# A hybrid decoder trunk on one NeuronCore: where on the queue the stored attention outputs come back, and which engine makes one sum

## The chip, the cores and the metric

One Trainium2 chip (trn2), one of its cores. The metric is the device time of one execution in microseconds (us), the median of several runs. The engines of the core are named as the profile names them: PE is TensorE (PEld its weight loads), DVE is VectorE, ACT is ScalarE, POOL is GpSimd, SP is SyncE, whose sequencer issues nearly all DMAs (SPq).

## The reference

Two layers on a sequence of 1024 tokens with 1024 features: a recurrent layer (RG-LRU) and a stick-breaking attention layer with 16 heads of 64, each followed by a dense feed-forward block. The change lies in attention:

```python
def stick_breaking_attention(x, w_qkv, w_o):
    qkv = jnp.einsum("bsd,de->bse", x, w_qkv).reshape(bsz, seq, 3, N_HEADS, HEAD_DIM)
    ...
    for blk in range(seq // Q_BLOCK):
        ...
        z = jnp.einsum("bhqd,bhkd->bhqk", qb, kb).astype(jnp.float32) * scale
        ...
        log_fail = jnp.where(strict, jax.nn.log_sigmoid(-z), 0.0)
        suffix = lax.cumsum(log_fail, axis=3, reverse=True) - log_fail
        weights = jnp.where(strict, jnp.exp(jax.nn.log_sigmoid(z) + suffix), 0.0)
        outs.append(jnp.einsum("bhqk,bhkd->bhqd", weights.astype(vb.dtype), vb))
    ...
    return jnp.einsum("bse,ed->bsd", o, w_o)
```

## The kernel before

**Tiles.** The activations lie transposed: 8 row blocks of 128 features (index k or d) by two column blocks of 512 tokens (index n). Each float32 matrix product is made of three matmuls of a high and a low part (mm3, lines 142 to 145). The input of attention lies in the tiles xh[k][n] and xl[k][n], 256 KB each. In the profile and in the listings below, these tiles carry the names of the buffers that they lie over: vh, vl or xg with numbers. xh[0][0] is vh0_3_2532 and xl[0][0] is vl0_3_2533; xh[1][0] and xl[1][0] are xg0_6477 and xg1_6478; xh[4][0] and xl[4][0] are vh2_3_2536 and vl2_3_2537.

**Attention.** The 16 heads go in 8 pairs (q from 0 to 7, NP = 8), each with its two heads hx. For each pair a projection makes q, k and v (which = 0, 1, 2) from all eight row blocks of xh and xl, for n = 0 and then n = 1 (qkv_steps; its matmuls write qk_ps). Each head has its score matmuls (z_ps, lines 1680 and 1681, in two PSUM buffers), a sigmoid on ScalarE (L1693), a running product on VectorE (scan, L1700 and L1703), and a transpose of the weights: partly by PE (wt_ps, L1725), with a cast th by ScalarE and a remainder tl by VectorE (L1734, L1735), partly by DMA (wt<-wx, L1714, whose operand wx ScalarE and VectorE write in L1710 and L1711). The matmuls av_ps (L1748) apply them. After each group a copy and an addition collect the two heads (oo, L1759 and L1760), add_v adds the values (oo<-oo,vt, L1764), and the result is split again into a high and a low part (L1771, L1772).

**Stored outputs.** The output of pair q belongs in row block q of the input of the next product, w_o. But xh and xl hold the input of attention until the last projection, that of v of pair 7. So the outputs of the first pairs are stored to DRAM (od[q, n]: odh and odl) and brought back into xh[q][n] and xl[q][n]. bring_back appends their two loads to a list, back.

**Order.** All five engines' orders are written out here. The loop over u runs through 192 units of work, 12 for each head, one step each: it carries out tasks whose time has come (due; stage(task, n) puts a task n steps ahead), issues one load from back (two in some of the last steps, L1870), makes scores and scans, then av_ps and transposes, then two steps of the running projection, and, from a few steps before pair 7's own heads, pieces of the product with w_o (out_fill, written as ob in the profile, then ob_ps). ob uses row blocks 0 to 6 of n = 0 in turn. SP's queue keeps the order in which the DMAs were written, and an instruction that waits holds up those behind it. Weight loads for what follows attention (raw<-in_attn_w_o, L116, 512 KB) are partly placed among them by the scheduler of the part behind.

The loads of pairs 0 to 5 are put on the list in the second half of evacuate, once the last projection of a column block n is complete (lines 1610 to 1612).

Of the kernel before, what the change touches and what calls it, by code (L numbers as in the profile page):

```python
# [34 lines left out]
def trunk(  # L35
# [21 lines left out]
    nc = tc.nc  # L57
# [84 lines left out]
    def mm3(ps, wh, wl, mh, ml, first, last, **kw):  # L142
        nc.tensor.matmul(ps, lhsT=wh, rhs=mh, start=first, stop=False, **kw)  # L143
        nc.tensor.matmul(ps, lhsT=wh, rhs=ml, start=False, stop=False, **kw)  # L144
        nc.tensor.matmul(ps, lhsT=wl, rhs=mh, start=False, stop=last, **kw)  # L145
# [1326 lines left out]
    NP = HEADS // 2  # L1472
# [15 lines left out]
    with ExitStack() as st:  # L1488
# [25 lines left out]
        def bring_back(*which):  # L1514
            for q, n in which:
                for x, dst in enumerate((xh, xl)):
                    back.append((f32(dst[q][n]), od[q, n][x]))


        def stage(task, steps=1):  # L1520
            soon.append([steps, task])

        def load_link(i):
            q, which = divmod(i, 3)
            if q < NP:
                raws[i] = load_raw(cols(w_qkv, which * D + q * P), (ND,))
            else:
                mix[0].load(which)
# [42 lines left out]
        def qkv_steps(q):  # L1571
            for which in range(3):
                w, at = wq.pop((q, which)), 3 * q + which + 1
                if at < 3 * NP:
                    raw = raws.pop(at)
                    wq[divmod(at, 3)] = next_weights(raw)
                    if which == 1:
                        later.extend(column_norms(raw, q))
                else:
                    mix[0].w[mix[0].order[0]] = next_weights(mix[0].raw.pop(0))  # L1580
                for i in (at + 1,) if at < 3 * NP else (at + 1, at + 2):
                    load_link(i)

                ks = (1, 5, 2, 6, 3, 7, 0, 4) if (q, which) == (0, 0) else range(ND)
                for n in range(NH):
                    pool, tag = (psZ, "z") if (q, which) == (0, 0) else (psQ, "qk")
                    ps = pool.tile([P, NB], F32, tag=tag, name="qk_ps")
                    for i, k in enumerate(ks):
                        mm3(ps, w[0][:, k], w[1][:, k], xh[k][n], xl[k][n], i == 0, i == ND - 1)
                        if i < ND - 1:  # L1590
                            yield
                    ev = evacuate(q, which, n, ps)
                    next(ev)
                    yield
                    next(ev, None)


        def evacuate(q, which, n, ps):
            full = lambda tag, m: [ap.tile([P, m, S], F32R, tag=tag, name=tag, bufs=4 if m == 1 else 3) for _ in range(2)]
            cs = slice(n * NB, (n + 1) * NB)  # L1600
            if which == 2:
                if n == 0:
                    VT[q] = ap.tile([P, S + 1], F32, tag="vt", name="vt", bufs=2)
                    nc.gpsimd.memset(VT[q][:, 0:1], 0.0)
                    VV[q] = ap.tile([P, 2, NT, 2, HD], F16, tag="v", name="v", bufs=2)
                t = ap.tile([P, NB], F32, tag="t", name="t", bufs=1)
                after = VT[q][:, n * NB + 1 : (n + 1) * NB + 1]
                nc.vector.scalar_tensor_tensor(after, ps, f32(sv[q]), rbc[n], op0=ALU.mult, op1=ALU.mult)
                yield
                if q == NP - 1:  # L1610
                    some = [(p, n) for p in range(NP - 2)]
                    bring_back(*some[:3], *([(NP - 2, 0)] * n), *some[3:])
                nc.vector.tensor_sub(t, VT[q][:, cs], after)
                vx = ap.tile([P, 4, 2, P], F16, tag="vx", name="vx", bufs=2)
                t3 = t.rearrange("p (b c) -> p b c", b=4)

                def low():
                    nc.vector.scalar_tensor_tensor(
                        vx[:, :, 1], t3, 1 / UP, vx[:, :, 0], op0=ALU.mult, op1=ALU.subtract
                    )  # L1620
                    for hx, a in enumerate((top, bot)):
                        nc.sync.dma_start(
                            VV[q][:, hx, 4 * n : 4 * n + 4].rearrange("p b h c -> p (b h) c"),
                            vx[a].rearrange("p b h c -> p (b h c)"),
                            transpose=True,
                        )
                def high():
                    nc.scalar.activation(vx[:, :, 0], t3, AF.Copy, scale=1 / UP)
                    stage(low)

                stage(high, 2)
                return
            two = ap.tile([P, 2, NB], F32R, tag="two", name="two", bufs=2)

            def spread():
                for hx, (a, b) in enumerate(((top, bot), (bot, top))):
                    if which == 0:
                        nc.sync.dma_start(f32(Q[q][hx])[a, cs], f32(two)[a, 0])
                        nc.sync.dma_start(f32(Q[q][hx])[b, cs], f32(two)[a, 1])
                    else:  # L1640
                        for half_ in (top, bot):
                            nc.sync.dma_start(f32(KK[q][hx])[half_, :, cs], f32(two)[a])

            def low():
                nc.vector.tensor_sub(two[:, 1], t, f32(two)[:, 0])
                stage(spread)

            if which == 0:
                t = ps
                if n == 0:  # L1650
                    Q[q] = [x[:, 0] for x in full("q", 1)]
                nc.scalar.copy(two[:, 0], t)
                yield
                low()
            else:
                t = f32(two)[:, 1]
                nc.vector.tensor_mul(t, ps, rbc[n])
                if n == 0:
                    KK[q] = full("kk", 2)
                yield  # L1660

                def high():
                    nc.scalar.copy(two[:, 0], t)
                    stage(low)

                stage(high)
# [73 lines left out]
        def av_part(tht, q, hx, G, kb, first, last):  # L1740
            q0 = (max(kb, 4 * G) - 4 * G) * P
            if first:
                av[0] = psO.tile([P, NB], F32, tag="o", name="av_ps")
            ps = av[0]
            if tht is None:
                tht = [T[q, hx][:, 2 * kb + x].rearrange("p j c -> p (j c)") for x in range(2)]
            for x, t in enumerate(tht):
                nc.tensor.matmul(  # L1748
                    ps[:, q0:], lhsT=VV[q][:, hx, kb], rhs=t[:, q0:], start=first and x == 0, stop=last and x == 1
                )  # L1750
            if not last:
                return
            a, b = (top, bot)[:: 1 if hx == 0 else -1]

            def gather():
                if hx == 0:
                    oo[q, G] = ap.tile([P, NB], F32, tag="oo", name="oo", bufs=2)
                o = oo[q, G]
                nc.scalar.copy(o[a], ps[b])  # L1759
                nc.vector.tensor_add(o[a], ps[a], o[a])  # L1760

            def add_v():
                eng = nc.vector if q >= NP - 2 else nc.gpsimd
                eng.tensor_add(oo[q, G], oo[q, G], VT[q][:, G * NB + 1 : (G + 1) * NB + 1])  # L1764

            def parts():
                o = oo[q, G]
                down = f32(av_[q])

                def both(hi, lo):  # L1770
                    nc.scalar.activation(hi, o, AF.Copy, scale=down)  # L1771
                    nc.vector.scalar_tensor_tensor(lo, o, down, f32(hi), op0=ALU.mult, op1=ALU.subtract)  # L1772

                if not kept(q, G):
                    both(xh[q][G], xl[q][G])
                else:
                    oh = ap.tile([P, NB], F32R, tag="oh", name="oh", bufs=1)
                    both(oh, o.bitcast(F32R))

                    def store():  # L1780
                        nc.sync.dma_start(od[q, G][0], f32(oh))
                        nc.sync.dma_start(od[q, G][1], o)

                    stage(store)

            later.insert(0, gather)
            if hx == 1:
                later.extend((add_v, lambda: None, parts))
# [32 lines left out]
        with tc.manual_schedule(engines={E.PE, E.Activation, E.DVE, E.Pool, E.SP}):  # L1821
# [39 lines left out]
            for u in range(-LEAD, len(units)):  # L1861
                some = chunks[c : c + 1]
# [92 lines left out]
```

## Time and profile before

| | us |
|---|---|
| median of 3 runs | 2152.64 |
| lowest and highest run | 2151.5, 2154.63 |
| the profiled execution | 2151.32 |
| its span, first to last instruction | 2149.3 |
| TensorE busy | 2127.2 (99% of the span) |
| VectorE busy | 1778.7 (83%) |
| ScalarE busy | 1136.3 (53%) |
| GpSimd busy | 129.0 (6%) |

Rows of the profile read: start in us from the span's start, duration in us, engine, line, operation, out<-in with the shape, how many were merged, and in brackets the idle time of the engine just before and what ended it. Rows of the waits read: who waited for whom, us in total, how often, the longest. In the rows of the stages, the pairs are busy time and count of PE, PEld, DVE, ACT and POOL, then the clock that TensorE was granted (1.00 is full), the mean busy share of the 16 DMA engines, and GB/s. A row of SPq is the issue of a DMA, not its transfer. GpSimd's additions of attention (L1764) are 12 in number with a mean of 1610 ns; the four that VectorE makes take 667 to 694 ns.

### The profile page before, as it was taken

What the parts mean: (1) busy time and instruction counts of PE and PEld (TensorE: products, weight loads), DVE (VectorE), ACT (ScalarE), POOL (GpSimd) and SP (SyncE); (2) the same over time, 40 slices, a digit from 0 to 9 for tenths busy, and PEclk for the clock granted to TensorE, in tenths of its full rate; (3) what the DMA queues carried; (4) which work ended last, traced back from release to release, by engine and by line L of the source; (5) the groups of instructions that cost most, each with busy time, mean ns of one, the idle gap of its engine ahead of it and who ended that gap; (6) DMA issues with size and microseconds to landing.
All of it is one profiled execution on the core that took longest, in us unless ns stands there. A gap on an engine that the chain in (4) does not pass through costs nothing. (4 is left out here: it accounts for less than half of the span.)

```text
span 2149.3 us, 28075 instructions
## 1 busy us (share of the span) xinstructions
PE 2127.2 (99%) x10158; PEld 1742.8 (81%) x10158; DVE 1778.7 (83%) x2609; ACT 1136.3 (53%) x1838; POOL 129.0 (6%) x100
## 2 busy tenths in 40 slices
PE   8999999999999999999999999899999999999998
PEld 7888888888888888888777777668888888888887
DVE  7887768888888888896899899877888888888886
ACT  6567435444444545564666666544544444454556
POOL 1222020000000000000000000002000000000002
PEclk9999999999999999999999999999999999999999
DMA  7111422334445774536667677972234444586442
GB/s 236 49 50 39 155 96 64 116 111 155 138 154 169 275 231 136 161 119 145 140 149 151 153 156 157 216 235 96 70 109 127 153 133 156 187 276 227 134 155 90
DMA packets 390314, 315.45 MB, mean 147 GB/s; under 512 B 101272, under 2 KB 296992, under 8 KB 390176
## 3 DMA queue, kind: packets, MB, share of 16 engines
q1 hardware_dynamic: 390016, 313.40, 49.9%
q8 instruction: 79, 1.29, 0.2%
q14 instruction: 59, 0.48, 0.1%
q10 hardware_dynamic: 160, 0.27, 0.0%
HBM read 184.09 MB, written 83.36 MB: 124 GB/s over the span
## 5 line engine op out<-in xcount | busy, mean ns | idle before, releaser
L143 PE MATMUL p_ps<-vh,wbh 128*128 128x512 f32 x524 | 204.9, 391 | 0.0
L144 PE MATMUL p_ps<-vl,wbh 128*128 128x512 f32 x524 | 204.5, 390 | 0.0
L143 PE MATMUL p_ps<-vh,wch 128*128 128x512 f32 x524 | 204.2, 390 | 0.0
L145 PE MATMUL p_ps<-vh,wcl 128*128 128x512 f32 x524 | 204.1, 389 | 0.0
L145 PE MATMUL p_ps<-vh,wbl 128*128 128x512 f32 x524 | 203.9, 389 | 0.0
L144 PE MATMUL p_ps<-vl,wch 128*128 128x512 f32 x524 | 203.9, 389 | 0.0
L722 ACT CAST wbh<-sb 128x1024 fp32r<-128x1024 f32 (+2 forms) x69 | 69.6, 1009 | 191.6 <-DVE sb L702 191.6
L1693 ACT ACTIVATE w<-z_ps,rs 128x128 f32<-128x128 f32 (+1 forms) x192 | 110.9, 580 | 100.1 <-PE z_ps L1681 99.8
L145 PE MATMUL p_ps<-vh,wal 128*128 128x512 f32 x396 | 154.0, 389 | 0.0
L143 PE MATMUL p_ps<-vh,wah 128*128 128x512 f32 x396 | 154.0, 389 | 0.0
L144 PE MATMUL p_ps<-vl,wah 128*128 128x512 f32 x396 | 154.0, 389 | 0.0
L1700 DVE TENSOR_TENSOR_SCAN w<-w,unit 128x128 f32<-128x128 f32 (+3 forms) x128 | 104.9, 830 | 17.4 <-ACT w L1693 17.1
L145 PEld LDWEIGHTS p_ps<-vh,wbl 128*128 128x128 f32 x524 | 98.4, 188 | 21.1
L145 PEld LDWEIGHTS p_ps<-vh,wcl 128*128 128x128 f32 x524 | 98.4, 188 | 21.0 <-DVE wcl L736 0.6
L144 PEld LDWEIGHTS p_ps<-vl,wch 128*128 128x128 f32 x524 | 98.4, 188 | 20.5
L143 PEld LDWEIGHTS p_ps<-vh,wch 128*128 128x128 f32 x524 | 98.3, 188 | 20.5 <-ACT tb L1181 0.2
L143 PEld LDWEIGHTS p_ps<-vh,wbh 128*128 128x128 f32 x524 | 98.6, 188 | 19.7 <-ACT U L1181 0.4
L144 PEld LDWEIGHTS p_ps<-vl,wbh 128*128 128x128 f32 x524 | 98.6, 188 | 18.5
L143 PE MATMUL qk_ps<-vh,whi 128*128 128x512 f32 x264 | 111.9, 424 | 0.0
L145 PE MATMUL qk_ps<-vh,wlo 128*128 128x512 f32 x264 | 103.6, 392 | 0.0
L144 PE MATMUL qk_ps<-vl,whi 128*128 128x512 f32 x264 | 103.3, 391 | 0.0
L143 PE MATMUL p_ps<-vh,wd 128*128 128x512 f32 x254 | 99.4, 391 | 0.1
(402 smaller groups left out, 5796.3 us busy)
## 6 DMA issues: line engine op xcount, KB each, us to landing
raw<-in_ffn_w_in SPq DMA_DIRECT2D x88, 512.0 KB, 4.1
vl<-pd SPq DMA_DIRECT2D x128, 256.0 KB, 3.5
pd<-U SPq DMA_DIRECT2D x90, 256.0 KB, 2.3
kk<-two SPq DMA_DIRECT2D x64, 256.0 KB, 4.5
raw<-in_ffn_w_out SPq DMA_DIRECT2D x56, 256.0 KB, 3.6
raw<-in_attn_w_qkv SPq DMA_DIRECT2D x24, 512.0 KB, 5.4
h<-hd SPq DMA_DIRECT2D x32, 256.0 KB, 5.4
hd<-h SPq DMA_DIRECT2D x32, 256.0 KB, 2.0
```

The lines of the kernel that those rows point to most:

```text
L143: nc.tensor.matmul(ps, lhsT=wh, rhs=mh, start=first, stop=False, **kw)
L144: nc.tensor.matmul(ps, lhsT=wh, rhs=ml, start=False, stop=False, **kw)
L145: nc.tensor.matmul(ps, lhsT=wl, rhs=mh, start=False, stop=last, **kw)
L722: nc.scalar.copy(self.full(self.wb), self.full(self.sb))
L1693: nc.scalar.activation(F, ps[:, 0:n], AF.Sigmoid, scale=rs[:, j : j + 1])
L1700: nc.vector.tensor_tensor_scan(rev, rev, unit[:, NB - n :][:, ::-1], 0.0, op0=ALU.mult, op1=ALU.add)
```

## The change

A stored row block k of column block n is now put on the list two steps after the last projection's matmuls for k and n were written, not for all k together when the projection of n is complete. Row block 6 of n = 0, which is stored late, follows block 3 of n = 1. And the addition of the values for pair 6 goes to GpSimd, like those of pairs 0 to 5; only pair 7's stays on VectorE.

```diff
@@ qkv_steps
                     for i, k in enumerate(ks):
                         mm3(ps, w[0][:, k], w[1][:, k], xh[k][n], xl[k][n], i == 0, i == ND - 1)
+                        if (q, which) == (NP - 1, 2):
+                            if k < NP - 2:
+                                stage(lambda k=k, n=n: bring_back((k, n)), 2)
+                            if (n, k) == (1, 3):
+                                stage(lambda: bring_back((NP - 2, 0)), 2)
                         if i < ND - 1:
                             yield
@@ evacuate
                 yield
-                if q == NP - 1:
-                    some = [(p, n) for p in range(NP - 2)]
-                    bring_back(*some[:3], *([(NP - 2, 0)] * n), *some[3:])
                 nc.vector.tensor_sub(t, VT[q][:, cs], after)
@@ add_v
-                eng = nc.vector if q >= NP - 2 else nc.gpsimd
+                eng = nc.vector if q == NP - 1 else nc.gpsimd
```

The order of PE's and ScalarE's instructions is the same in both kernels. SP's queue before, from the transpose for which SP waits at 1365.63 us to the load of the second row block (kk is the keys of pair 7; v the transposes of its values):

```order
L1714 DMA_TRANSPOSE wt_12375<-wx_12372 128x8x128
L1642 DMA kk_12224<-two_12294 64x2x512 x2
L1642 DMA kk_12225<-two_12294 64x2x512 x2
L1714 DMA_TRANSPOSE wt_12375<-wx_12413 128x8x128
L1714 DMA_TRANSPOSE wt_12375<-wx_12438 128x8x128
L1870 DMA vh0_3_2532<-odh0_0_7885 128x512
L1714 DMA_TRANSPOSE wt_12375<-wx_12480 128x8x128
L1870 DMA vl0_3_2533<-odl0_0_7886 128x512
L1622 DMA_TRANSPOSE v_12429<-vx_12445 128x8x64 x2
L1870 DMA xg0_6477<-odh1_0_7887 128x512
L1870 DMA xg1_6478<-odl1_0_7888 128x512
```

The same place of the changed kernel:

```order
L1872 DMA vh0_3_2532<-odh0_0_7885 128x512
L1716 DMA_TRANSPOSE wt_12376<-wx_12373 128x8x128
L1644 DMA kk_12224<-two_12294 64x2x512 x2
L1644 DMA kk_12225<-two_12294 64x2x512 x2
L1872 DMA vl0_3_2533<-odl0_0_7886 128x512
L1716 DMA_TRANSPOSE wt_12376<-wx_12415 128x8x128
L1872 DMA xg0_6477<-odh1_0_7887 128x512
L1716 DMA_TRANSPOSE wt_12376<-wx_12441 128x8x128
L1872 DMA xg1_6478<-odl1_0_7888 128x512
L1716 DMA_TRANSPOSE wt_12376<-wx_12483 128x8x128
L1872 DMA vh4_3_2540<-odh2_0_7889 128x512
L1624 DMA_TRANSPOSE v_12431<-vx_12448 128x8x64 x2
```

The first load moved ahead of all four transposes, its partner ahead of three, and the loads of the second row block stand among them.

SP's queue before, around the loads of the fifth row block (vh2 and vl2; odh6 and odl6 are stores of pair 6):

```order
L1870 DMA xg9_7656<-odl3_0_7892 128x512
L116 DMA raw_13150<-in_attn_w_o 128x8x128
L1622 DMA_TRANSPOSE v_12429<-vx_12554 128x8x64 x2
L1781 DMA odh6_0_7897<-oh_12581 128x512
L1782 DMA odl6_0_7898<-oo_12213 128x512
L1870 DMA vh2_3_2536<-odh4_0_7893 128x512
L1870 DMA vl2_3_2537<-odl4_0_7894 128x512
L1870 DMA xg4_6481<-odh5_0_7895 128x512
```

And in the changed kernel:

```order
L1872 DMA xg9_7656<-odl3_0_7892 128x512
L1872 DMA vh2_3_2536<-odh4_0_7893 128x512
L1872 DMA vl2_3_2537<-odl4_0_7894 128x512
L1872 DMA xg4_6481<-odh5_0_7895 128x512
L1624 DMA_TRANSPOSE v_12431<-vx_12557 128x8x64 x2
L1783 DMA odh6_0_7897<-oh_12584 128x512
L1784 DMA odl6_0_7898<-oo_12213 128x512
L1872 DMA xg5_6482<-odl5_0_7896 128x512
```

The three loads moved ahead of the transposes and stores, and the weight load raw_13150 is gone from here; it now stands behind the last of the loads that come back, between the transposes of the last head.

GpSimd's queue at the end of attention, as the difference of the two (vt are the values, wlo a part of a weight):

```order
 L1548 TENSOR_SCALAR sv<-nh 128x1
 L1549 TENSOR_SCALAR av<-nh 128x1
-L1604 MEMSET vt 128x1
+L1609 MEMSET vt 128x1
+L1766 TENSOR_TENSOR oo<-oo,vt 128x512 x2
 L1559 TENSOR_TENSOR wlo<-raw,whi 128x512 x2
```

Two additions are new there. On VectorE the two rows oo<-oo,vt of pair 6 are gone, and nothing else of its order is different.

## The prediction

> **What bounds the kernel now.** First the page's list of engines, then the waits of TensorE between 1370 and 1425 us, the stretch in which attention ends and the stored outputs come back.
>
> ```profile
> PE 2127.2 (99%) x10158; PEld 1742.8 (81%) x10158; DVE 1778.7 (83%) x2609; ACT 1136.3 (53%) x1838; POOL 129.0 (6%) x100
> ...
> PE ob L144 <- DMA vl<-odl: 2.7, 2, 2.4
> PE ob L143 <- DMA vh<-odh: 2.7, 2, 2.4
> PE av_ps L1748 <- DVE tl L1735: 2.2, 4, 0.8
> PE av_ps L1748 <- ACT th L1734: 2.2, 2, 1.7
> ```
>
> TensorE (PE) is busy 99% of the span, so the change can win only where PE stands or runs slowly. Here it stands 5.4 us for loads of the stored outputs (columns of the waits: us in total, times, longest). Next the busy time by stage; behind the engines stand the granted clock, the share of the DMA engines and GB/s.
>
> ```profile
> 1363.40:1366.90 3.50, 3.50 (x19) 2.42 (x18) 3.28 (x6) 2.99 (x7) 1.62 (x3) 1.00 0.02 5
> 1366.90:1381.00 14.10, 11.47 (x64) 8.61 (x62) 14.04 (x23) 7.82 (x17) 0.00 (x0) 1.00 1.04 202
> 1381.30:1384.70 3.40, 3.40 (x11) 1.87 (x10) 3.15 (x6) 2.97 (x5) 0.00 (x0) 0.50 0.88 235
> ...
> 1391.10:1394.90 3.80, 1.09 (x4) 0.49 (x4) 3.39 (x7) 1.70 (x4) 0.00 (x0) 1.00 0.99 282
> 1394.90:1398.30 3.40, 3.40 (x12) 2.37 (x12) 0.78 (x2) 1.04 (x4) 0.00 (x0) 0.50 1.14 258
> 1398.30:1410.00 11.70, 10.35 (x59) 6.81 (x58) 11.39 (x18) 7.87 (x16) 0.00 (x0) 1.00 1.02 333
> 1421.00:1440.00 19.00, 19.00 (x93) 14.40 (x92) 11.36 (x17) 8.81 (x14) 0.00 (x0) 1.00 0.84 266
> ```
>
> Three things stand in it. Two stretches of 3.4 us have half the clock, each just behind a wait for a load. VectorE (DVE, third pair) is full almost everywhere: 14.04 of 14.10, 11.39 of 11.70. It has real holes only where PE stood for the second load. And the DMA engines are free from 1363.4 to 1366.9 and then full until 1410. After 1421 PE never stops (19.00 of 19.00), so whatever is won by then stays won.
>
> So the question is which engine ends the waits at each place. PE's rows:
>
> ```profile
> 1380.92 0.51 PE L144 MATMUL ob<-vl,whi 128*128 128x512 f32 x1 [2.43 <-DMA vl<-odl]
> ...
> 1382.71 0.80 PE L1680 MATMUL z_ps<-kk,q 128*128 128x512 f32 x1
> ...
> 1393.52 0.49 PE L143 MATMUL ob<-vh,whi 128*128 128x512 f32 x1 [2.40 <-DMA vh<-odh]
> ...
> 1397.04 0.85 PE L1725 MATMUL wt_ps<-ident,w 128*128 128x128 f32 x3
> ...
> 1381.56 0.63 ACT L1628 ACTIVATE vx<-t 128x512 f16<-128x512 f32 x1 [3.38 <-DVE t L1613]
> 1382.10 0.56 ACT L1693 ACTIVATE w<-z_ps,rs 128x384 f32<-128x384 f32 x1
> ...
> 1401.87 0.73 ACT L1771 ACTIVATE vh<-oo,av 128x512 fp32r<-128x512 f32 x1
> ```
>
> The score matmul z_ps at 1382.71 needs one of two PSUM buffers, which the sigmoid at 1382.10 empties (it ends at 1382.66). That sigmoid is queued behind vx, which waits for DVE's t. **So the first wait hides a second one**: with its load early, PE would run on for about 1.8 us and stand at the score matmul until 1382.5. The second wait has no such thing behind it. VectorE's rows:
>
> ```profile
> 1379.13 1.22 DVE L1700 TENSOR_TENSOR_SCAN w<-w,unit 128x512 f32<-128x512 f32 x1
> 1380.26 0.67 DVE L1764 TENSOR_TENSOR oo<-oo,vt 128x512 f32<-128x512 f32 x1
> 1380.84 0.69 DVE L1613 TENSOR_TENSOR t<-vt 128x512 f32<-128x512 f32 x1
> ...
> 1390.52 1.16 DVE L1735 TENSOR_TENSOR tl<-wt_ps,th 128x512 f16<-128x512 f32 x2 [0.36 <-ACT th L1734]
> ...
> 1398.12 0.62 DVE L1735 TENSOR_TENSOR tl<-wt_ps,th 128x256 f16<-128x256 f32 x2 [2.62 <-ACT th L1734]
> ...
> 1399.37 0.69 DVE L1760 TENSOR_TENSOR oo<-av_ps,oo 64x512 f32<-64x512 f32 x1
> ...
> 1400.97 0.67 DVE L1764 TENSOR_TENSOR oo<-oo,vt 128x512 f32<-128x512 f32 x1
> 1401.67 1.16 DVE L1735 TENSOR_TENSOR tl<-wt_ps,th 128x512 f16<-128x512 f32 x2
> ...
> 1404.19 0.73 DVE L1772 SCALAR_TENSOR_TENSOR vl<-oo,av,vh 128x512 fp32r<-128x512 f32 x1
> ```
>
> VectorE is idle 0.36 and 2.62 us for th, ScalarE's cast of PE's transposed weights, which PE made late because it stood for loads. Those holes, not PE's 5.4 us, are what earlier loads can win.
>
> **The change part by part. The loads.** Their number and size stay; they move on SP's one queue.
>
> ```profile
> 1356.85 2.42 SPq L116 DMA_DIRECT2D raw<-in_attn_w_o  x2
> 1365.63 1.26 SPq L1714 DMA_TRANSPOSE wt<-wx  x1
> ...
> 1375.46 1.26 SPq L1714 DMA_TRANSPOSE wt<-wx  x1
> 1376.77 0.57 SPq L1870 DMA_DIRECT2D vl<-odl  x1
> ...
> 1383.45 0.42 SPq L116 DMA_DIRECT2D raw<-in_attn_w_o  x1
> ...
> 1389.79 0.39 SPq L1870 DMA_DIRECT2D vh<-odh  x1
> ```
>
> SP stands from 1359.3 (1356.85 + 2.42) to 1365.63 for that transpose's operand. The first load now stands ahead of it, so it goes out at about 1359.3 and falls into the free 3.5 us. Its partner passes two transposes. That ends the 2.43 us wait, but by the rows above PE then stops at 1382.5 instead of 1382.7: nearly nothing. The fifth pair, issued at 1389.79, passes the 512 KB weight load of 1383.45, two transposes and two stores; it takes the weight load's place behind the fourth pair, so it is issued at about 1383.5, 6 us earlier. Needed at 1391.1 (1393.52 - 2.40), or some 2 us before that in a schedule that runs ahead, it has 5 to 7 us to land; vl at 1376.77 took 4.1 (to 1380.92). So the 2.40 us wait ends. The weight load goes to the back, where nothing of PE's needs it before 1421.
>
> *(a) holes.* 0.36 at 1390.52 (bounds 0 and 0.36). Of the 2.62 at 1398.12 I take 2.55, as the casts still follow a wait of ScalarE for the scan ahead (bounds 0, should the pair land late, and 2.62). Cover: PE's transposes of 1397.04 come 2.4 us earlier without the wait, and 1.0 or more without the half clock around them: at 1393.6 or before. VectorE, working without holes, gets to tl only at about 1395. So a load may be 1.4 us late there at no cost, and beyond that costs what it is late.
>
> **The sum on GpSimd.** Two additions of 0.67 us leave VectorE; the same additions of earlier heads show what they do there.
>
> ```profile
> 1323.43 0.75 DVE L1608 SCALAR_TENSOR_TENSOR vt<-qk_ps,sv,rbc 128x512 f32<-128x512 f32 x1
> 1323.48 1.10 POOL L1764 TENSOR_TENSOR oo<-oo,vt 128x512 f32<-128x512 f32 x1 [13.36 <-DVE oo L1760]
> ...
> 1324.09 1.56 DVE L1700 TENSOR_TENSOR_SCAN w<-w,unit 128x512 f32<-128x512 f32 x1
> 1325.58 0.66 DVE L1613 TENSOR_TENSOR t<-vt 128x512 f32<-128x512 f32 x1
> ...
> 1341.48 2.12 POOL L1764 TENSOR_TENSOR oo<-oo,vt 128x512 f32<-128x512 f32 x1 [16.90 <-DVE oo L1760]
> ...
> 1342.63 1.52 DVE L1711 TENSOR_TENSOR wx<-w,wx 128x512 f16<-128x512 f32 x1
> ```
>
> *(b) first addition.* Beside it the scan took 1.56 instead of 1.22. From scan to t it was 1325.58 - 1324.09 = 1.49 with the sum on GpSimd; now it is 1380.84 - 1379.13 = 1.71. Won: 0.22 (bounds 0 and 0.58, the slot of the addition). The instructions of VectorE around it are the same ones, so 0.22 it is.
>
> *(c) second addition.* Its slot is 1401.67 - 1400.97 = 0.70. GpSimd took 2.12 in the like place, and a two-input operation beside it 1.52 where it takes about 0.68: up to 0.84 given back. VectorE's next instruction here reads PSUM, like vt at 1323.43, which was not stretched. So less is given back than that: won 0.45 (bounds -0.14 and 0.70). The sum is also ready later: GpSimd ends 2.12 after oo is ready, against 1401.64 - 1400.06 = 1.6 now, so ScalarE's vh (1401.87) and the casts queued behind it slip by 0.5. VectorE reads vh only at 1404.19, 1.6 after it is written, which hides that; without this cover it costs 0.5.
>
> A rule of the Trainium skill speaks against this edit: its page "SBUF — State Buffer", section "SBUF: two separate sides", says that VectorE with two SBUF inputs and GpSimd exclude one another for a whole instruction. By it both additions cost VectorE about what they free, and the sum below would lose 0.6; the stretched scan agrees in kind, at 0.34 of it.
>
> *(d) half clock.* The two half-clock stretches are charged to the holes only as far as they fell on them in this execution. Where they lie relative to the waits can differ from run to run; half of 3.4 us is 1.7 us for one that is all in the way, and I add a quarter of it, 0.4 (bounds 0 and 1.7).
>
> "TensorE: Matmul & The Clock Gate" in the Trainium skill, section "Part 1: The HAM clock gate", has the clock halved after an idle window of about 3.4 us. The rows show it behind waits of 2.4 us, so the measurement decides; by the page's number term (d) would be 0.
>
> **Sum:** 0.36 + 2.55 + 0.22 + 0.45 + 0.4 = 3.98, about 4.0 us. The profiled execution took 2151.3 us (its span is 2149.3), so 2147.3 for it. It lies 1.3 us under the median of the runs, 2152.64, from which the forecast is **2148.6 us**.
>
> **The rivals.** *All of PE's loss comes back.* 5.4 us of waits and two half-clock stretches (3.4 us lost) are 8.8 us: 2143.8. For it: PE is 99% busy. Against: VectorE's 14.04 of 14.10 and the score matmul behind the first wait. It holds if VectorE catches up faster than its rows say.
>
> *The loads land no earlier.* From 1366.9 on the DMA engines are full, and a new order moves no more bytes. Then one load in the free stretch, (b) and (c) are left: about 1.0 us, 2151.6. Against: what the fifth pair passes is 512 KB and four other transfers, which nobody awaits.
>
> *Slower: transposes pushed back.* Transposes two to four of the head in work there now stand behind one, two and three loads. If each holds the full queue for half of vl's 4.1 us (an estimate), three take 6.2, and the fourth transpose goes out at 1375.46 + 6.2 = 1381.7 and lands 4.1 later, at 1385.8. PE takes it just behind the score matmul of 1382.5, at about 1383. It decides from there: PE would stand 2.8 us and lose 1.7 more at half clock, the holes of (a) would stay, and the end would be 2157.1. Against: the load itself costs SP only 0.57, and with that alone the transpose lands at 1381.3, 1.7 us in time.
>
> **How the numbers follow.** Forecast 0.59, full recovery 0.15, no earlier 0.18, transposes 0.08. The forecast's own range is 2147.0 to 2150.2. The range 2145.0 to 2153.0 takes in the no-earlier case and some of the full recovery; it leaves out the transposes and the rest. A measurement of this kernel can tell about 0.2%, 4.3 us, from no change; that line is at 2148.3, just beside the forecast. Faster: 0.15 and about half of 0.59, 0.43. Slower: most of the last case, 0.07. Within: 0.50.
>
> **What would show it.** Right: no TensorE wait of ob for a load over 0.5 us at the first pair, and in its place a wait of z_ps of some 2.5 to 3 us that ends at about 1382.5; no hole over 0.3 us of VectorE ahead of tl between 1385 and 1400; the tl of 1398.12 at about 1395; GpSimd additions of about 1.1 and 2.1 us, the scan beside the first at about 1.55; attention's last matmuls some 4 us earlier. The forecast is wrong if PE's av_ps waits for a transpose, if the fifth pair is still awaited for over 1.5 us, or if a new wait of VectorE for ScalarE stands around 1398, behind the second sum.

## The result and the profile after

| | before | after |
|---|---|---|
| median, us | 2152.44 (22 runs) | 2148.89 (22 runs) |
| lowest and highest run | 2149.77, 2155.22 | 2146.85, 2151.5 |
| the profiled execution, and its span | 2151.32, 2149.3 | 2150.7, 2148.9 |

The ratio is 0.9983, with a 95% interval of 0.9977 to 0.9990: 3.55 us, 0.17%, won. That is clear of no change, and just under the 0.2% (2148.3 us) that the prediction set as its line. The forecast was 2148.6 us, its own range 2147.0 to 2150.2, and the time lies in it. The wide range, 2145.0 to 2153.0, is little of a test, since it takes in the time of the kernel before.

The two profiled executions are only 0.6 us apart, since they are not typical ones: the one of before lies 1.1 us under its median, the one of after 1.8 us above. The one of after was already 1.15 us late at the last projection, long before the change has any effect (the matmul at 1344.26 starts at 1345.41), and lost another 0.6 us behind attention, at about 2112 us. All times of after around 1370 to 1420 are therefore to be read minus 1.15.

First, the engines and the waits of TensorE between 1370 and 1425 us in the profile after (who waited for whom: us in total, times, the longest).

```profile
PE 2126.3 (99%) x10158; PEld 1741.3 (81%) x10158; DVE 1778.8 (83%) x2607; ACT 1135.9 (53%) x1838; POOL 125.6 (6%) x102
...
PE z_ps L1682 <- ACT w L1695: 3.6, 3, 2.9
PE ob L143 <- DMA vh<-odh: 2.4, 1, 2.4
PE av_ps L1750 <- DVE tl L1737: 1.9, 3, 0.9
PE ob L144 <- DMA xg<-odl: 1.0, 1, 1.0
```

The loads are awaited for 3.4 us instead of 5.4, and at other places; the wait of z_ps for ScalarE's sigmoid was 0.2 us before and is 3.6 now. The stages, cut as before (busy time and count of PE, PEld, DVE, ACT and POOL, clock, DMA share, GB/s):

```profile
1363.40:1366.90 3.50, 3.50 (x19) 2.37 (x18) 3.31 (x6) 2.87 (x6) 1.71 (x3) 1.00 0.64 201
1366.90:1381.00 14.10, 13.60 (x74) 10.31 (x72) 13.97 (x23) 8.94 (x19) 1.09 (x1) 1.00 1.03 214
1381.30:1384.70 3.40, 1.09 (x5) 0.68 (x6) 3.15 (x6) 2.25 (x5) 0.00 (x0) 1.00 0.68 154
...
1394.90:1398.30 3.40, 2.94 (x20) 1.95 (x19) 2.92 (x7) 3.35 (x8) 0.21 (x1) 1.00 1.34 276
1398.30:1410.00 11.70, 7.46 (x32) 3.76 (x32) 10.98 (x16) 6.84 (x15) 1.59 (x1) 0.96 0.98 282
```

The free 3.5 us of the DMA engines are now used (0.64 instead of 0.02). Both half-clock stretches are gone from their places. VectorE works in 1394.9 to 1398.3, where it had done 0.78. But PE has lost ground in 1398.3 to 1410 (7.46 instead of 10.35), and its clock is 0.96 there: a new half-clock stretch begins at 1409.13. PE's and ScalarE's rows show why:

```profile
1379.24 0.40 PE L143 MATMUL ob<-vh,whi 128*128 128x512 f32 x1
...
1383.61 0.50 PE L1682 MATMUL z_ps<-kk,q 128*128 128x512 f32 x1 [2.91 <-ACT w L1695]
...
1390.00 0.39 PE L143 MATMUL ob<-vh,whi 128*128 128x512 f32 x1
...
1407.41 0.50 PE L143 MATMUL ob<-vh,whi 128*128 128x512 f32 x1 [2.43 <-DMA vh<-odh]
...
1382.45 0.63 ACT L1630 ACTIVATE vx<-t 128x512 f16<-128x512 f32 x1 [3.13 <-DVE t L1615]
1382.99 0.56 ACT L1695 ACTIVATE w<-z_ps,rs 128x384 f32<-128x384 f32 x1
...
1399.92 0.72 ACT L1773 ACTIVATE vh<-oo,av 128x512 fp32r<-128x512 f32 x1 [0.80 <-POOL oo L1766]
```

The first and the fifth pair are no longer awaited at all (1379.24, 1390.00), and PE stands 2.91 us at z_ps instead, until 1382.46 on the clock of before, as foretold. The wait at 1407.41 was not: it is for row block 6. VectorE's and GpSimd's rows:

```profile
1380.28 1.56 DVE L1702 TENSOR_TENSOR_SCAN w<-w,unit 128x512 f32<-128x512 f32 x1
1381.76 0.66 DVE L1615 TENSOR_TENSOR t<-vt 128x512 f32<-128x512 f32 x1
...
1391.15 1.16 DVE L1737 TENSOR_TENSOR tl<-wt_ps,th 128x512 f16<-128x512 f32 x2
1392.22 1.28 DVE L1713 TENSOR_TENSOR wx<-w,wx 128x512 f16<-128x512 f32 x2
...
1396.07 0.62 DVE L1737 TENSOR_TENSOR tl<-wt_ps,th 128x256 f16<-128x256 f32 x2
1396.61 0.68 DVE L1702 TENSOR_TENSOR_SCAN w<-w,unit 128x256 f32<-128x256 f32 x1
...
1398.04 0.96 DVE L1702 TENSOR_TENSOR_SCAN w<-w,unit 128x384 f32<-128x384 f32 x1
1399.03 1.16 DVE L1737 TENSOR_TENSOR tl<-wt_ps,th 128x512 f16<-128x512 f32 x2
...
1413.61 1.16 DVE L1737 TENSOR_TENSOR tl<-wt_ps,th 128x512 f16<-128x512 f32 x2 [2.14 <-ACT th L1736]
...
1379.67 1.09 POOL L1766 TENSOR_TENSOR oo<-oo,vt 128x512 f32<-128x512 f32 x1 [13.36 <-DVE oo L1762]
1398.09 1.80 POOL L1766 TENSOR_TENSOR oo<-oo,vt 128x512 f32<-128x512 f32 x1 [17.33 <-DVE oo L1762]
```

The holes of 0.36 and 2.62 us ahead of tl are gone. A hole of 2.14 stands ahead of a later tl that had 0.55: PE stood for row block 6, so its transposes and ScalarE's th came late.

### The profile page after: what moved, and what is told of

It is laid out like the page before. It is cut to its first block, busy times and chain, and to the rows that moved or that the text cites. A ratio compares the mean times of both kernels' runs of the same rounds, so it can differ in the third digit from the quotient of the medians.

```text
span 2148.9 us, 28075 instructions
## 1 busy us (share of the span) xinstructions
PE 2126.3 (99%) x10158; PEld 1741.3 (81%) x10158; DVE 1778.8 (83%) x2607; ACT 1135.9 (53%) x1838; POOL 125.6 (6%) x102
## 4 chain that ended last, share of the span: by engine, by line
PE 95%; DVE 2%; DMA 1%; issue 1%; ACT 1%; SPq 0%; DVEq 0%; ACTq 0%
PE p_ps L143 18%; PE p_ps L145 18%; PE p_ps L144 18%; PE qk_ps L143 4%; PE qk_ps L145 4%; PE qk_ps L144 4%; PE av_ps L1750 3%; PE a_ps L144 3%; PE a_ps L145 3%; PE a_ps L143 3%; PE ob_ps L143 3%; PE ob_ps L145 3%; PE ob_ps L144 3%; PE z_ps L1682 1%; PE z_ps L1683 1%; PE wt_ps L1727 1%
```

## The experiments

Two instructions that every kernel has serve as a ruler: the matmul at 1344.26 in the profile before, and the tl that starts there at 1414.67. Their distance is called the **stage** below. It leaves out what differs between profiles elsewhere. Behind that tl the same matmul (1435.24 before) follows after 20.54 to 20.58 us in ten of the 14 profiles; in the other four a half-clock stretch lies behind tl, and it is 22.13 to 22.18. So, half clock aside, the end moves with the start of that tl.

| kernel | median, us | ratio to before, 95% | stage, us |
|---|---|---|---|
| before | 2152.44 | 1 | 70.41; again 69.75 |
| first pair early alone | 2151.77 | 0.9999 (0.9990 to 1.0008) | 69.77 |
| sum alone | 2151.48 | 0.9997 (0.9988 to 1.0006) | 69.44 |
| fifth pair early alone | 2150.32 | 0.9989 (0.9979 to 0.9998) | 69.24 |
| loads alone | 2150.69 | 0.9988 (0.9979 to 0.9997) | 67.75 |
| the change | 2148.89 | 0.9983 (0.9977 to 0.9990) | 68.20 |
| the change, again | 2148.50 | 0.9981 (0.9972 to 0.9990) | 67.38 |
| row block 6 early | 2148.40 | 0.9980 (0.9971 to 0.9989) | 67.72 |
| row block 6 early, again | 2148.86 | 0.9982 (0.9973 to 0.9991) | 66.61 |
| the same, sum on VectorE | 2149.87 | 0.9986 (0.9978 to 0.9995) | 67.57 |
| row block 6 early, vx later | 2148.47 | 0.9980 (0.9972 to 0.9989) | 66.24 |
| the same, wlo on GpSimd | 2148.59 | 0.9981 (0.9972 to 0.9990) | 65.28 |
| row block 6 early, tl thrice | 2152.98 | 1.0001 (0.9992 to 1.0010) | 70.80 |

Medians are compared with runs of the kernel before beside them, whose medians were 2152.7 to 2153.0.

**The loads without the sum.**

```diff
-                eng = nc.vector if q == NP - 1 else nc.gpsimd
+                eng = nc.vector if q >= NP - 2 else nc.gpsimd
```

> The changed kernel with the addition of pair 6 left on VectorE. Theory A: the gain is VectorE's two holes ahead of tl, closed by the loads, and the new 2.4 us wait of ob for vh of pair (6, 0) near 1407 hides what the sum brings. Then this is within 0.4 us of the change, 2148.9 to 2149.3, with no hole of VectorE over 0.4 us between 1385 and 1400, and the wait for (6, 0) is shorter by about 0.7 us (1.7 instead of 2.4). Rival B: the sum's 0.7 us comes on top of the loads' gain and reaches the end: 2149.6. Rival C: the sum on GpSimd is most of the gain: over 2150.5.

```profile
1408.28 0.50 PE L143 MATMUL ob<-vh,whi 128*128 128x512 f32 x1 [1.02 <-DMA vh<-odh]
```

VectorE has no hole over 0.41 us between 1385 and 1400. The stage is as long as the change's (67.75 against 68.20 and 67.38), and the wait for row block 6 is 1.02 us instead of 2.43; but in the second profile of the change it is 1.31, so the sum need not be the reason. The median itself, 2150.69, is over C's 2150.5; but the runs of the kernel before beside it were slower too (2153.04), and the ratio, 0.9988, gives the loads 0.0012 of the change's 0.0017. With the sum alone at 0.9997 (below) C falls. A and B are not told apart, as the intervals overlap widely. By the medians, what the loads do is most of the change.

**The sum without the loads**, the same line edited in the kernel before.

> The kernel before with the addition of pair 6 moved to GpSimd and nothing else. Theory A: the first addition's time goes into the holes that VectorE has anyway ahead of tl near 1390 and 1398 (2.62 becomes about 2.8), and only what stands behind the last hole counts, at most 0.45: 2152.0. Rival C: the sum is most of the gain, about 3 us: 2149.5. Rival D (the two engines shut each other out, as a page of the notes has it): nothing to 0.6 us slower, 2152.4 to 2153.0. A and D are told apart by the slot of the second addition: the time from VectorE's scan ahead of it to the tl behind it falls by 0.4 to 0.7 under A, by nothing under D.

```profile
1400.10 0.62 DVE L1735 TENSOR_TENSOR tl<-wt_ps,th 128x256 f16<-128x256 f32 x2 [1.90 <-ACT th L1734]
...
1402.08 0.96 DVE L1700 TENSOR_TENSOR_SCAN w<-w,unit 128x384 f32<-128x384 f32 x1
1403.07 1.16 DVE L1735 TENSOR_TENSOR tl<-wt_ps,th 128x512 f16<-128x512 f32 x2
```

From scan to tl it takes 0.99 us. With the addition in between it took 1.57 in the kernel before, where that scan stands at 1400.10 and the tl at 1401.67:

```profile
1400.10 0.96 DVE L1700 TENSOR_TENSOR_SCAN w<-w,unit 128x384 f32<-128x384 f32 x1
```

So 0.58 leave VectorE, and D, by which this slot would stay, falls at this place. C falls by the time, 0.9997. The hole at 1400.10 is 1.90, shorter than the 2.62 of the first profile of before, not longer as expected, and the first addition's 0.2 us is too little to be seen in it.

**Row block 6 earlier.**

```diff
-                            if (n, k) == (1, 3):
+                            if (n, k) == (1, 0):
                                 stage(lambda: bring_back((NP - 2, 0)), 2)
```

> The changed kernel, but with row block 6 of n = 0 put on the list behind block 0 of n = 1 instead of block 3; its loads are issued at about 1393 instead of 1402 and should land at about 1398. Theory A: the wait of ob for it (2.4 us at 1407.4) and the half clock of 1409.1 to 1412.6 cost about 1.6 us; both go, and VectorE's hole of 2.14 us at 1413.6 goes to under 0.7: 2147.3. Rival E: VectorE is the bound behind it as well, PE then stands about as long at the next tl or transpose: within 0.4 us of the change, 2148.5 to 2149.3. Rival F: two more loads ahead of three transposes of the last head push these back, and av_ps waits for one: over 2150.

This and its repetition are read together below.

**Only the first pair early.** Empty places in the list keep every other load where it was.

```diff
+                        if (q, which, n, k) == (NP - 1, 2, 0, 0):
+                            stage(lambda: bring_back((0, 0)), 2)
...
-                    some = [(p, n) for p in range(NP - 2)]
-                    bring_back(*some[:3], *([(NP - 2, 0)] * n), *some[3:])
+                    if n == 0:
+                        back.extend([[], []])
+                        some = some[1:]
...
```

> The kernel before with only the first pair of loads (row block 0, n = 0) moved to where the change has it; every other DMA and every sum stands as before. Theory A (the first wait hides a second one): PE stands about 2.5 to 3 us at z_ps instead of 2.4 us at ob, until about 1382.5, and the fifth pair is awaited as before: 2152.0 to 2152.4, at most 0.4 us won. Rival G: PE's wait was all loss, so its 2.4 us and part of a half-clock stretch come back: 2149.0 to 2150.0.

```profile
1378.84 0.40 PE L144 MATMUL ob<-vl,whi 128*128 128x512 f32 x1
...
1383.22 0.50 PE L1687 MATMUL z_ps<-kk,q 128*128 128x512 f32 x1 [3.16 <-ACT w L1700]
...
1393.60 0.50 PE L143 MATMUL ob<-vh,whi 128*128 128x512 f32 x1 [1.96 <-DMA vh<-odh]
```

The first pair is not awaited, PE stands 3.16 us at z_ps, the fifth pair is awaited as before, and the time is unchanged. The first wait hid the second one, as the prediction had it; G falls.

**Only the fifth pair early.**

```diff
+                    if n == 0:
+                        for i in (6, 7):
+                            back[i] += back[i + 2]
+                            back[i + 2] = []
...
```

> The kernel before with only the fifth pair of loads (row block 4, n = 0) brought forward, by two steps, ahead of the transposes and stores and of the weight load, which goes to the back; the other loads and the sums stand as before. Theory A: this pair makes the 2.40 us wait of ob at about 1393 and VectorE's hole of 2.62 us ahead of tl at 1398; both go, and the stage ends about 2.5 us earlier: 0.9988 of the kernel before (0.9980 to 0.9993). Rival G: PE's waits count one for one, so the first pair is worth as much as the fifth. Rival H: the gain needs both pairs early, since PE arrives late otherwise: under 1 us here.

```profile
1384.60 1.22 DVE L1704 TENSOR_TENSOR_SCAN w<-w,unit 128x512 f32<-128x512 f32 x1 [0.59 <-ACT w L1697]
...
1388.61 1.28 DVE L1707 TENSOR_TENSOR_SCAN w<-w,w 128x512 f32<-128x512 f32 x1 [1.01 <-ACT w L1697]
...
1396.68 0.62 DVE L1739 TENSOR_TENSOR tl<-wt_ps,th 128x256 f16<-128x256 f32 x2
...
1381.77 0.80 PE L144 MATMUL ob<-vl,whi 128*128 128x512 f32 x1 [3.31 <-DMA vl<-odl]
```

The median is A's: 0.9989, about 2.4 us. Its interval (0.4 to 4.5 us) takes in H as well, and overlaps with that of the first pair alone. In the profile the hole at tl is gone (1396.68), but the stage is only 0.5 to 1.2 us shorter, nearer to H: PE's wait for the first pair was longer here, 3.31 us, 6.8 us at half clock began in it (at 1380.63), and VectorE then waited 0.59 and 1.01 us at places where it otherwise does not. PE also stood 1.61 us for the second load of row block 5. So the two pairs are not simply additive: the early first pair buys nothing by itself, but without it a wait can end in half clock and open holes again. One profile does not say how often.

**The wait at z_ps taken away.** Row block 6 early, and:

```diff
-                stage(high, 2)
+                stage(high, 3 if (q, n) == (NP - 1, 1) else 2)
```

> As the kernel in which row block 6 comes back behind block 0 of n = 1, and ScalarE's vx of the last values is put one step later, behind the two sigmoids that it held up (its remainder on VectorE and its two transposes follow one step later). Nothing is left out. PE's wait of 2.9 us at z_ps near 1383.5 goes. Theory A (VectorE bounds this stretch): the end of the stage moves by at most 0.5 us, apart from half-clock stretches that do or do not occur; PE's standing turns up at later places (av_ps for tl). Rival G (PE's waits are the loss): 2.9 us faster, about 0.9967 of the kernel before.

```profile
1382.62 0.71 PE L1750 MATMUL av_ps<-wt,v 128*128 128x512 f16 x2 [2.06 <-DMA wt<-wx]
```

PE's 2.9 us at z_ps are gone, and PE stands 2.06 us for a transpose instead. The time is that of the kernel without this edit (0.9980). The stage is 0.4 us shorter than in that kernel's better profile (66.24 against 66.61). That a wait goes at one place and comes up at another, with the same time, is what A foretold. Against G the run is weak by itself, since PE's standing fell by less than a microsecond (2.06 for 2.9). A wait of av_ps for a transpose, which the prediction named as a sign against it, comes up here without a longer stage; in the change itself there is none.

**More work on VectorE.** Row block 6 early, and the four tl of one group computed three times:

```diff
+            for _ in range(3 if (q, hx, G) == (NP - 1, 0, 0) else 1):
                 nc.vector.tensor_sub(tl[:, q0:], tp[:, q0:], th[:, q0:])
```

> As the kernel in which row block 6 comes back behind block 0 of n = 1, with four tl of pair 7's first head computed three times instead of once: eight more instructions on VectorE, 3.2 us by their slots in that run (0.61 + 0.46 and 0.34 + 0.19, twice), between 1392 and 1399. Theory A (VectorE bounds this stretch): its few holes behind (0.41, 0.55, 0.69 us) swallow up to 1 us and the rest arrives at the end, 2.2 to 3.2 us slower than that kernel. Rival G (PE bounds): the matmuls that wait for these tl slip, others fill in, under 1 us slower.

```profile
1390.33 3.79 DVE L1738 TENSOR_TENSOR tl<-wt_ps,th 128x512 f16<-128x512 f32 x6
1394.03 1.28 DVE L1713 TENSOR_TENSOR wx<-w,wx 128x512 f16<-128x512 f32 x2
...
1397.87 2.19 DVE L1738 TENSOR_TENSOR tl<-wt_ps,th 128x256 f16<-128x256 f32 x6
1399.98 0.68 DVE L1702 TENSOR_TENSOR_SCAN w<-w,unit 128x256 f32<-128x256 f32 x1
```

From the first tl to what follows each group it takes 3.70 and 2.11 us instead of the 1.07 and 0.54 of single ones (in after, 1391.15 to 1392.22 and 1396.07 to 1396.61): 4.2 us more. The slots were estimated a fourth too small, so the 2.2 to 3.2 us expected were too few. The stage grew by 4.19 against the profile of that kernel without holes behind half clock (70.80 against 66.61), by 3.08 against the other (67.72). The time grew by 0.0019 to 0.0021 of the whole, 4.1 to 4.5 us, with intervals that do not meet. **Work added to VectorE reaches the end almost whole.** VectorE's last holes for ScalarE (0.41, 0.68 and 0.55 us) did not swallow it; they are as long as without it. This is the clearest result, for A.

**The sum, with row block 6 out of the way.** Row block 6 early, pair 6's addition on VectorE.

> As the kernel in which row block 6 comes back behind block 0 of n = 1, with the addition of pair 6 left on VectorE. With the wait for row block 6 out of the way, the sum is no longer hidden by it. Theory A: this is 0.5 to 0.9 us slower than with the sum on GpSimd, and the slots show it: from scan to t 1.7 instead of 1.5, from the scan ahead of the second addition to the tl behind it 0.7 more. Rival D (the engines shut each other out): no difference in the slots.

The stage is 67.57 us: 0.96 longer than 66.61, the profile with one half-clock stretch like this one, but not longer than 67.72, the profile with two. The time is 1.0 to 1.5 us longer in the medians, with overlapping intervals. From scan to tl:

```profile
1397.72 0.96 DVE L1702 TENSOR_TENSOR_SCAN w<-w,unit 128x384 f32<-128x384 f32 x1
...
1399.29 1.16 DVE L1737 TENSOR_TENSOR tl<-wt_ps,th 128x512 f16<-128x512 f32 x2
```

1.57 again, and 0.98 in the kernel with the sum on GpSimd; from scan to t it is 1.72 (1379.58 to 1381.30). So the slots are as A has them, and D, which had no difference in them, falls. The times alone would not show it.

**The change, before and row block 6 early, each again.**

> The changed kernel once more, for a second profile of it and more runs beside the variant with row block 6 early. In ten profiles so far the half-clock stretches lie on a grid of 3.41 us, each behind a grid window in which PE was busy 0.57 or less, and the grid's phase differs from run to run. Theory A: the wait for row block 6 (2.4 us, give or take 0.5) and VectorE's hole behind it at tl near 1413 are there again, since a landing time sets them; the half clock may fall elsewhere; 0.998 to 0.999 of the kernel before. Rival J: the wait was an accident of the first profile and is under 1 us now.

> The kernel before, a second profile. Theory A: the waits for the first and the fifth pair (together 4.4 to 5.6 us) and VectorE's holes ahead of tl (1.9 to 2.7 us at about 1398) are there again, and the time from the first head's last projection (the matmul at 1344.26) to the tl at 1414.67, 70.4 us in the first profile, is between 69.5 and 71.

> Row block 6 behind block 0 of n = 1, once more. Theory A: no wait of ob for row block 6, VectorE's hole at tl near 1413 at 0.55, and the time from the projection's matmul to that tl 66.8 to 67.8 us (67.72 with 0.89 us of holes behind two half-clock stretches in the first profile, 66.8 without); against the change run beside it 0.5 to 1.5 us faster. Rival E: no faster than the change.

The change, then row block 6 early (its loads' first issue on SP, the matmul that uses them, and the tl behind):

```profile
1405.82 0.50 PE L143 MATMUL ob<-vh,whi 128*128 128x512 f32 x1 [1.31 <-DMA vh<-odh]
...
1412.02 1.16 DVE L1737 TENSOR_TENSOR tl<-wt_ps,th 128x512 f16<-128x512 f32 x2 [1.03 <-ACT th L1736]
```

```profile
1394.12 0.82 SPq L1872 DMA_DIRECT2D vh<-odh  x1
...
1405.37 0.39 PE L143 MATMUL ob<-vh,whi 128*128 128x512 f32 x1
...
1412.58 1.16 DVE L1737 TENSOR_TENSOR tl<-wt_ps,th 128x512 f16<-128x512 f32 x2 [0.55 <-ACT th L1736]
```

The wait for row block 6 is no accident of one profile, 2.43 and 1.31 us, though the second lies between what A and J expected; the hole behind it is 2.14 and 1.03. Early loads end both. But A's 2147.3 did not come (2148.40 and 2148.86), and the gain is small: over two profiles each, the matmul of 1435.24 comes 88.77 and 87.95 us behind the ruler's first in the change, 88.27 and 87.19 with row block 6 early, 0.6 us less on average. The first of the latter had 6.8 us at half clock, with 0.49 and 0.40 us of VectorE waiting for ScalarE behind it. The times do not tell them apart (0.9983 and 0.9981 against 0.9980 and 0.9982), and in the last batch, side by side, row block 6 early had a median 0.36 us above the change's, so that rival E can't be excluded, and that this version beats the change is not shown. The kernel before, again, waited 2.85 us for the first pair and 1.58 for the fifth, but its holes were smaller than expected (0.40 and 0.38 us ahead of tl, 1.06 ahead of a scan, between 1392 and 1401); the stage was 69.75, as expected. By the means of two profiles each, the stage is 2.3 us shorter in the change than before, and the same matmul comes 3.1 us earlier (88.36 against 91.45), as a half-clock stretch lay behind tl in the second profile of before. The times have 3.55.

**Two more sums off VectorE.** As the kernel with vx later, and:

```diff
-                    mix[0].w[mix[0].order[0]] = next_weights(mix[0].raw.pop(0))
+                    mix[0].w[mix[0].order[0]] = next_weights(mix[0].raw.pop(0), nc.gpsimd)
```

> Row block 6 early, vx one step later, and the two wlo of the first w_o weights (0.66 us each on VectorE at 1371.7 and 1374.9) on GpSimd as well. Nothing is left out. Theory A (VectorE bounds this stretch): 1.3 us leave VectorE, 0.3 us come back for each as a stretched neighbour: 0.7 us faster than without it by the stage's length, near 65.5 us from the projection's matmul to the tl of 1411 (66.24 without); in the times about 0.9977 of the kernel before. Rival G: nothing gained, since PE's own waits stay.

The stage is 65.28 us, 0.96 less, where A expected about 0.7: VectorE again. The times do not move (0.9981). In this profile and in the one with vx later, a half-clock stretch lies behind tl and gives 1.6 us back; whether that is chance or follows from the earlier tl stays open. No version is shown to beat the change.

## Why the prediction came true, point by point

- **VectorE bounds, and the first wait hides a second.** Right, and shown: the first pair alone gives 0.9999 and a wait at z_ps, and 4.2 us of extra work on VectorE make the stage 3.1 to 4.2 us longer. VectorE is not alone on the path: in every profile it waits 0.41 and 0.68 or 0.69 us ahead of wx, and at least 0.55 ahead of the ruler's tl, for ScalarE. Whether faster casts there would win is untested.
- **(a) The holes, 2.91 us.** The two holes ahead of tl are gone, and the tl of 1398.12 comes at 1394.92 on the clock of before (1396.07 less 1.15); about 1395 was said. In the second profile of before the comparable holes sum to 1.8, so the term is 2 to 3 us, and its first profile was at the upper end. Up to the tl behind the second addition (1401.67), (a), (b) and (c) make 3.58; it came 3.79 us earlier in the first pair of profiles (1399.03 less 1.15), 2.84 in the second (53.92 us behind the ruler's first against 56.76). What closes the smaller hole is open: with the first pair alone early it is still there, at 0.36.
- **(b) and (c) The sum, 0.22 and 0.45.** From scan to t it is now 1.48 against 1.71: 0.23. The second slot won 0.58, for the scan beside GpSimd kept its 0.96, and GpSimd paid with 1.80 instead of 1.09. A scan and such an addition do not run at once: the second addition needed 0.89 us more once the scan had ended (1399.00 to 1399.89), and at about 1342 in the two profiles of the change either the scan of 1.28 us took 2.22 beside an addition of 1.09, or it kept 1.28 and the addition took 2.13. The two tl behind the second addition, which read one operand from PSUM, kept their 1.16. The rule of the Trainium skill's page "SBUF — State Buffer", section "SBUF: two separate sides", has VectorE instructions with two SBUF inputs and a GpSimd instruction that reads SBUF wait for one another, and these rows agree with it. What does not follow from it is the prediction's estimate by that rule, that the sum would lose 0.6 us: the first scan met only the last 0.48 us of the addition (1380.28 to 1380.76), and in the second slot it was GpSimd that stood. ScalarE's vh starts 1.88 us behind the scan ahead of the sum (1398.04 to 1399.92), against 1.77 before (1400.10 to 1401.87): 0.1 late, not 0.5.
- **(d) Half clock, 0.4.** By the profiles not settled: the change has one and two such stretches in its two, before has two and two. But every run has its mean granted clock: on average 0.9974 in the 93 runs of before beside the experiments, 0.9986 in the 33 of the change. That is 2.6 us of clock less lost, or 1.5 stretches of 3.41 us at half clock. Among the 93 runs those at 0.996 took 1.9 us longer on average than those at 0.998 (2154.05 against 2152.14), for 4.3 us of clock. At that rate the 2.6 us are worth about 1.1, an estimate, and by it the term was too small. Why there are fewer such stretches is not shown.
- **The fifth pair** was issued at 1384.28, as said within a microsecond, and is not awaited. No transpose is awaited by av_ps.
- **What the prediction did not see: row block 6.** The change puts its pair one place further back on the list. The part on the loads costed the first and the fifth pair and never asked what the next load in line would do once VectorE and PE run 4 us ahead. SP issues its first load at 1402.02 before, 5.4 us ahead of its use, and at 1402.25 after:

```profile
1402.02 0.42 SPq L1870 DMA_DIRECT2D vh<-odh  x1
...
1407.43 0.39 PE L143 MATMUL ob<-vh,whi 128*128 128x512 f32 x1
```

```profile
1402.25 0.42 SPq L1872 DMA_DIRECT2D vh<-odh  x1
```

In before it was used without a wait at 1407.43; PE now wants it at 1404.98 (1407.41 - 2.43) and gets it at 1407.41. The chain of work that ended last, followed back in the profile after, runs through this pair: its second load takes 5.33 us from 1402.71, then come ob at 1408.09, th at 1412.99 and the tl at 1413.61. In the second profile of the change the chain holds the same load, with 4.42 us. The hole ahead of that tl, 0.55 and 0.56 in the two profiles of before, grew to 2.14 and 1.03, so 1.59 and 0.47 us of what had been won were lost again, and the stage is 2.21 and 2.37 us shorter. "Attention's last matmuls some 4 us earlier" did not come true: the matmul of 1435.24 comes 2.2 us earlier in the first pair of profiles, and of the 4.0 in the second 1.6 are the half-clock stretch of before.

- **The number.** 3.55 us were won in the times (2.2 to 5.0 by the interval) against 3.98 in the sum. The stage accounts for 2.3 of them in the profiles. Fewer stretches of half clock, about 1.1 by the estimate above, can be the rest, though the two may overlap. So the forecast came near in part by luck: it left out the wait for row block 6 (some 0.6 us by the profiles of the kernel without it), and something of about that size, which the stage does not show, made up for it. The profiled execution took 2150.7, not 2147.3: about 1.8 us of the difference arose outside the stage, the rest in it.
- **The rivals.** Full recovery, 2143.8, falls. Loads no earlier falls: the first and the fifth pair are not awaited, and the loads alone give 0.9988. Transposes pushed back falls: av_ps waits for none in the change. Nor does a new wait of VectorE for ScalarE stand behind the second sum (the tl of 1399.03 has none).

## What to carry to other kernels

An engine that is 99% busy need not be the one that sets the end: add a known amount of work to the suspected engine, and see how much of it reaches the end. A wait that ends earlier is worth only what the bounding engine was idle for it; ask who is idle, not who waits. And when a stretch is made shorter by some microseconds, go through every later load that was just in time, for each of them is now late by as much; the reordered list itself must be read to its end, not only at the places where waits were.

## What the runs showed of the hardware

PE's granted clock changes on a fixed grid. In all 14 profiles the half-clock stretches between 1370 and 1425 us are 3.41 us long or twice that, and begin on a grid of 3.41 us whose place against the program differs from run to run. Two neighbouring windows of that grid in the change, and two in the kernel with row block 6 early, again (busy time of PE is the second number, the clock stands third from the end):

```profile
1405.72:1409.13 3.41, 1.54 (x5) 1.05 (x6) 2.73 (x4) 1.21 (x2) 0.00 (x0) 1.00 1.03 383
1409.13:1412.55 3.42, 3.42 (x10) 1.63 (x9) 2.34 (x3) 1.83 (x3) 1.55 (x1) 0.50 0.51 114
```

```profile
1416.25:1419.66 3.41, 1.55 (x11) 1.33 (x11) 2.14 (x5) 2.12 (x5) 0.00 (x0) 1.00 1.21 217
1419.66:1423.08 3.42, 3.42 (x19) 2.33 (x19) 2.06 (x5) 1.60 (x5) 0.00 (x0) 1.00 1.19 301
```

Behind every window that ran at full clock with PE busy for less than 0.45 of it, the next ran at half clock; from 0.45 to 0.57 it went either way (1.54 of 3.41 us did, 1.55 did not), and from 0.60 on it never did. So where a wait falls on the grid matters: PE stood 2.91 us at z_ps in the profile of the change at full clock, and the same 2.90 us in its second profile were followed by a half-clock stretch. What a stretch cost where PE was the one to wait for can be read behind the ruler's tl, 22.13 to 22.18 us instead of 20.54 to 20.58, or 1.6 us. The Trainium skill's page "TensorE: Matmul & The Clock Gate", section "Part 1: The HAM clock gate", has a free-running window, and the grid agrees with it. It also has the clock halved after an idle window; here a window in which PE was busy for 1.54 of 3.41 us was enough, and the measurement decides.
